# The last norm of a hybrid decoder layer: order of the left half's multiplications, sum of the last squares, and the queue of the last transfers

## The chip, the core and the metric

The kernel runs on one core of a Trainium2 chip. The metric is the device time of one execution in microseconds (us). The core has five engines that take their own instructions in order: TensorE (PE in the profile; its weight loads are PEld), VectorE (DVE), ScalarE (ACT), GpSimd (POOL) and SyncE (SP). SP computes nothing here; it issues the DMA transfers. Engines wait for one another through semaphores.

## What is computed

The reference is one decoder layer over 1024 tokens and 1024 channels. Only its end matters here: the down projection of the MLP is added to the residual, and a norm over the channels of each token follows.

```python
    x = x + (jax.nn.silu(gate) * up) @ w_down
...
    y = xf * lax.rsqrt(jnp.mean(xf * xf, axis=-1, keepdims=True) + EPS)
    return (y * w.astype(jnp.float32)).astype(x.dtype)
```

The kernel keeps the result transposed: channels lie on the 128 partitions, in eight channel tiles `m` = 0 to 7, and tokens lie along the free dimension. So the mean over the channels of a token is a sum over the eight tiles and then over the partitions.

## The kernel before

Most of the kernel is matrix products in three parts (a number is split into a high and a low half, and three products of halves are added). The order of work is written out by hand with the help of a planner, `Weave`, which interleaves streams of work by estimated times; every operation goes through the recorder `Engine`, so that VectorE, ScalarE and GpSimd operations carry line L139 (those of the high-priority recorder L141), and all matrix products carry L189 (function `mm`) or, for transposes through the identity, L193 (function `tp`). On each engine the instructions run in the order in which they are written, as far as this end of the kernel goes.

The MLP's down projection is the function `mlp_down`. It works in four stages with 11 steps each; the tokens are halved (`hh` = 0 is tokens 0 to 511) and the output channels are halved into tiles 0 to 3 and 4 to 7. The last stage makes channel tiles 4 to 7 of token half 0, with four PSUM banks `pa[0]` to `pa[3]` (named `dw` in the trace). By then everything of token half 1 is done, and its last norm is interleaved with the stage. The last five steps of the stage are held back and done bank by bank by `last_product(i, sl)`: 15 matrix products into one bank for 256 tokens `sl`, then `add_to` (VectorE adds the bank to the residual `x1h[4 + i]`), then `complete` (ScalarE squares the sum into `sq`, and VectorE adds the square to `rstdB`, which collects the squares of all eight channel tiles).

The 512 tokens are taken as **left** (0 to 255) and **right** (256 to 511). The order is: the left products of all four banks; the right product of bank 0; then `final_norm(0, left, ...)`, with the right product of bank 1 between its power and its transposes; the right products of banks 2 and 3; and `final_norm(0, right, ...)`.

`final_norm` has these steps: for each 128 tokens a matrix product of `rstdB` with a column of ones (the sum over the partitions); a VectorE multiply and add (`rs`); a power of -1/2 on GpSimd (`rsqrt`); transposes on TensorE that turn the column of 128 factors into a row that stands on all partitions (bank `pb`); and then, for each of the eight channel tiles, one VectorE multiplication (SCALAR_TENSOR_TENSOR) by the norm's weight and by that row, and one transfer of 128 x 256 numbers (128 KB) to the output, `out_xT`, issued by SP. The end of the program waits for the transfers.

So before the change the eight left multiplications stand on VectorE between the add of right bank 1 and the adds of right banks 2 and 3. The right norm's sum over the partitions needs the right squares of all four banks in `rstdB`.

A transfer on the SP queue waits for the multiplication that made its data and for an earlier transfer that used the same one of eight completion semaphores.

Of the kernel before, what the change touches and what calls it, by code (L numbers as in the profile page):

```python
# [7 lines left out]
F32 = mybir.dt.float32  # L8
F32R = mybir.dt.float32r
AF = mybir.ActivationFunctionType  # L10
OP = mybir.AluOpType
# [4 lines left out]
P = 128  # L16
# [8 lines left out]
EPS = 1e-6  # L25
# [119 lines left out]
def hybrid_layer(tc, I, out):  # L145
    nc = tc.nc
    wv = Weave()
    ve = Engine(wv, nc.vector, "vector", 0.07, 0.00105)
    ac = Engine(wv, nc.scalar, "scalar", 0.12, 0.00085)

    uv = Engine(wv, nc.vector, "vector", 0.07, 0.00105, first=tc.high_priority)
    ua = Engine(wv, nc.scalar, "scalar", 0.12, 0.00085, first=tc.high_priority)
    po_ = Engine(wv, nc.gpsimd, "gpsimd", 0.15, 0.0021)
    sy = Engine(wv, nc.sync, "sync", 0.05, 0.00142, 2.2)
    es = ExitStack()
    cp = es.enter_context(tc.tile_pool(name="cp", bufs=1))
    wp = es.enter_context(tc.tile_pool(name="wp", bufs=1))
    lp = es.enter_context(tc.tile_pool(name="lp", bufs=1))
    sp = es.enter_context(tc.tile_pool(name="sp", bufs=1))
# [3 lines left out]
    def tile_(pool, shape, dt, name, tag, bufs):  # L163
        return wv.slot(pool.tile(list(shape), dt, name=name, tag=tag, bufs=bufs), tag, bufs)
# [3 lines left out]
    def A(name, tag, dt=F32, shape=(P, 1024)):  # L168
        if tag in TURNS:
            i = turns[tag] = turns.get(tag, -1) + 1  # L170
            tag = TURNS[tag][i % len(TURNS[tag])]
        return tile_(lp, shape, dt, name, tag, SLOTS[tag])
# [4 lines left out]
    def const(name, shape, src=None):  # L177
        t = cp.tile(list(shape), F32, name=name)
        if src is not None:
            sy.dma_start(t, src)  # L180
        return t
# [3 lines left out]
    def after(inst, anchor, reason="keeps a slot free until it is needed"):  # L185
        tc.add_manual_dep(inst.ins, anchor.ins.name, order, reason=reason)

    def mm(dst, lhs, rhs, us, start=True, stop=True, **kw):
        tc.stamp_issue_order_token(nc.tensor.matmul(dst, lhs, rhs, start=start, stop=stop, **kw).ins, TOKEN)  # L189
        wv.product(us, dst, lhs, rhs)  # L190

    def tp(dst, src, idt=None, us=0.11):
        tc.stamp_issue_order_token(nc.tensor.transpose(dst, src, ident if idt is None else idt).ins, TOKEN)  # L193
        wv.product(us, dst, src)
# [33 lines left out]
    def rsqrt(dst, src, n):  # L228
        po_.tensor_tensor(dst, src, mhalf[:, :n], op=OP.pow)
# [14 lines left out]
    def bank(tag, name="ps"):  # L244
        return tile_(pp_, (P, 512), F32, name, tag, 2)
# [26 lines left out]
    for k in range(KT):  # L272
# [24 lines left out]
        sq = A("sq", "qa")  # L297
# [5 lines left out]
        else:  # L303
            inst = ve.tensor_tensor(acc, acc, sq, op=OP.add)
# [7 lines left out]
    ones = const("ones", [P, 8])  # L312
# [36 lines left out]
    rstdB = const("rstdB", [P, S])  # L349
# [697 lines left out]
    last = {}  # L1047
# [30 lines left out]
    fw = const("fw", [P, KT], I["fw"])  # L1078
# [259 lines left out]
    x1h = {}  # L1338
# [70 lines left out]
    def load_x1(mg, hh):  # L1409
        for m in range(4 * mg, 4 * mg + 4):  # L1410
            if not hh:
                x1h[m] = A("x1h", ("kT", "kT", "dv", "dv", "Xa", "Xa", "Xa", "Xa")[m])
            sy.dma_start(x1h[m][:, half(hh)], xpark[m][:, half(hh)])

    def down(pd, i, op, sl, first, last_):
        (whi, wlo), (hhi, hlo) = op
        c = slice(i * P, (i + 1) * P)
        mm3(pd[:, sl], (whi[:, c], wlo[:, c]), (hhi[:, sl], hlo[:, sl]), first, last_, skip_group_check=True)

    def part(m, hh, sl):  # L1420
        return slice(512 * hh + sl.start, 512 * hh + sl.stop)

    def add_to(pd, m, hh, sl):
        x = x1h[m][:, part(m, hh, sl)]
        ve.tensor_tensor(x, x, pd[:, sl], op=OP.add)

    def complete(m, hh, sl):

        sp_ = part(m, hh, sl)
        x = x1h[m][:, sp_]  # L1430
        sq = tile_(sp, [P, 512], F32, "sq3", "t2", 2)
        ac.activation(sq[:, sl] if m else rstdB[:, sp_], x, AF.Square)
        if m:
            ve.tensor_tensor(rstdB[:, sp_], rstdB[:, sp_], sq[:, sl], op=OP.add)

    def final_norm(hh, sl, tags, between=None):
        n_ = (sl.stop - sl.start) // P
        ss = bank(tags[0])
        for c in range(n_):
            o = 512 * hh + sl.start + c * P  # L1440
            mm(ss[:, c:c + 1], rstdB[:, o:o + P], ones[:, :1], 0.215)
        rs = tile_(sp, [P, 4], F32, "rs3", "rs3", 2)
        ve.tensor_scalar(rs[:, :n_], ss[:, :n_], 1.0 / 1024, EPS, op0=OP.mult, op1=OP.add)
        rsqrt(rs[:, :n_], rs[:, :n_], n_)
        if between is not None:
            between()
        pb = bank(tags[1])
        for c in range(n_):
            tp(pb[:, c * P:(c + 1) * P], rs[:, c:c + 1].to_broadcast([P, P]))
        for m in range(8):  # L1450
            x = x1h[m][:, part(m, hh, sl)]
            ve.scalar_tensor_tensor(x, x, fw[:, m:m + 1], pb[:, :sl.stop - sl.start], op0=OP.mult, op1=OP.mult)
            sy.dma_start(out[m * P:(m + 1) * P, part(m, hh, sl)], x)

    STEPS = [(s_, j) for s_ in range(4) for j in range(HT)]
    XLOADS = {6: (0, 0), 12: (1, 0), 14: (0, 1), 16: (1, 1)}
# [3 lines left out]
    def mlp_down():  # L1460
        yield from wv.until("up")
        whole = slice(0, 512)
        pa = [bank(t, "dw") for t in ("asc", "atr") for _ in range(2)]
        pb = [bank(t, "dw") for t in ("hf", "ch") for _ in range(2)]
        def down_step(stage, j):
            for e, (op, pds) in enumerate(zip(ops[stage, j], (pa, pb))):
                for i in range(4):
                    down(pds[i], i, op, whole, j == 0 and (stage == 0 or (stage, e) == (1, 1)), j == HT - 1)
                if j == HT - 1:
                    mg, hh = ADDS[stage][e]  # L1470
                    for i in range(4):
                        add_to(pds[i], 4 * mg + i, hh, whole)
                        if stage == 0 and e == 1:
                            complete(i, 0, whole)
                        if stage == 2 and e == 1:
                            complete(i, 1, whole)
                    if stage == 2 and e == 1:
                        for i in range(4):
                            complete(4 + i, 1, whole)

        for n, (stage, j) in enumerate(STEPS):
            if n + 1 < len(STEPS):
                prep(*STEPS[n + 1])
            if n in XLOADS:
                load_x1(*XLOADS[n])
            if stage == 3 and j == HT - LAST - 1:
                final_norm(1, whole, ("hf", "ch"), lambda: down_step(stage, j))
            elif stage < 3 or j < HT - LAST:
                down_step(stage, j)

        def last_product(i, sl):
            for j in range(HT - LAST, HT):
                down(pa[i], i, ops[3, j][0], sl, False, j == HT - 1)
            add_to(pa[i], 4 + i, 0, sl)
            complete(4 + i, 0, sl)


        left, right = slice(0, 256), slice(256, 512)
        for i in range(4):
            last_product(i, left)  # L1500
        last_product(0, right)
        final_norm(0, left, ("hf", "ch"), lambda: last_product(1, right))
        for i in (2, 3):
            last_product(i, right)
        final_norm(0, right, ("hf", "ch"))

    wv.add(0, norms())
    wv.add(1, gates())
# [6 lines left out]
    wv.add(0, mixer_splits())  # L1515
    wv.add(8, mlp_up())
    wv.add(8, mlp_down())
    wv.run()
    es.close()
# [58 lines left out]
```

## Time and profile before

| | us |
|---|---|
| median of 3 runs (lowest to highest) | 1223.74 (1222.77 to 1223.82) |
| the profiled execution, its own time | 1223.87 |
| span of that execution, first to last instruction | 1222.1 |
| TensorE busy in the span | 1201.4 |
| VectorE busy | 950.3 |
| ScalarE busy | 574.5 |
| last product of right bank 3 ends | 1210.35 |
| first of the last eight multiplications starts | 1214.85 |
| last of the eight transfers is issued | 1218.74 |

The times of day in the text (1210.35 and so on) are microseconds from the span's start. What the profiled execution takes beside its span, 1223.87 - 1222.1, is outside the first and last instruction. A row of the timeline gives the start, the length from first to last of a merged group, the engine, line and operation, `out<-in`, the count after `x`, and in brackets how long the engine was idle before and what released it. Rows of the same kind are merged when nothing of that engine lies between them, so the length of one is read from the start of the next, or from a narrow window.

### The profile page before, as it was taken

The numbers are of one execution on the slowest core, as the hardware profiler recorded it, in microseconds if no ns is written. First come the engines' busy times: TensorE is split into PE (matmuls) and PEld (weight loads), VectorE is DVE, ScalarE is ACT, GpSimd is POOL, SyncE is SP. The second block draws the span as 40 slices with busy tenths as digits, with TensorE's granted clock in tenths as the row PEclk, the third lists the DMA queues.
The fourth block names the chain that finished last, engine by engine and source line by source line (L and its number), as shares of the span: only waits on it lengthen the run. The fifth ranks groups of instructions, "written<-read, shape, count | busy, mean of one in ns | idle before, by whom it ended". The sixth has DMA issues, their size and how long they took to land.

```text
span 1222.1 us, 18237 instructions
## 1 busy us (share of the span) xinstructions
PE 1201.4 (98%) x7064; PEld 986.3 (81%) x7064; DVE 950.3 (78%) x1458; ACT 574.5 (47%) x1123; POOL 50.1 (4%) x46
## 2 busy tenths in 40 slices
PE   9999999999999999999999999999999999999996
PEld 7878887889777778788888888888888888787886
DVE  7675965566487686668988988989889889899875
ACT  7393344356344453555545544445444444343441
POOL 0211010003100000000000000000000000000000
PEclk9999999999999999999999999999999999999998
DMA  7425252335634213444223123132231496555623
GB/s 228 110 74 168 77 148 88 118 126 163 215 105 121 88 37 101 157 147 155 71 68 104 58 98 99 57 104 65 91 101 55 142 369 238 165 164 181 193 81 138
DMA packets 85799, 154.81 MB, mean 127 GB/s; under 512 B 21168, under 2 KB 36304, under 8 KB 85712
## 3 DMA queue, kind: packets, MB, share of 16 engines
q1 hardware_dynamic: 85712, 153.64, 39.3%
q8 instruction: 55, 0.90, 0.3%
q14 instruction: 32, 0.26, 0.1%
HBM read 117.68 MB, written 35.93 MB: 126 GB/s over the span
## 4 chain that ended last, share of the span: by engine, by line
PE 84%; DVE 8%; DMA 3%; issue 2%; ACT 2%; SPq 0%; POOLq 0%; POOL 0%; DVEq 0%; ACTq 0%
PE ps L189 43%; PE pa L189 20%; PE pc L189 10%; PE dw L189 8%; PE ps L193 3%; DMA wd<-in_wd 3%; DVE pr L139 2%; DVE x1h L139 1%; DVE kT L139 1%; DVE wd L139 1%; ACT dec L139 1%; DMA xt<-in_xT 1%; DVE wlo L139 0%; DVE r L139 0%; ACT sq L141 0%
## 5 line engine op out<-in xcount | busy, mean ns | idle before, releaser
L189 PE MATMUL dw<-pr 128*128 128x512 f32 (+1 forms) x984 | 213.4, 378 | 3.3 <-DVE x1h L139 3.1
L189 PEld LDWEIGHTS dw<-pr 128*128 128x128 f32 x984 | 176.2, 188 | 39.5 <-DVE x1h L139 4.8
L189 PE MATMUL ps<-xhi,whi 128*128 128x512 f32 x384 | 158.7, 413 | 0.0
L189 PE MATMUL ps<-xlo,whi 128*128 128x512 f32 x384 | 150.2, 391 | 0.6 <-DVE xlo L139 0.6
L189 PE MATMUL ps<-xhi,wlo 128*128 128x512 f32 x384 | 150.4, 392 | 0.0
L189 PE MATMUL pa<-T,pair 128*128 128x512 f32 x528 | 127.1, 390 | 0.0
L189 PEld LDWEIGHTS pa<-T,pair 128*128 128x128 f32 x528 | 99.0, 188 | 20.5
L189 PEld LDWEIGHTS ps<-xhi,wlo 128*128 128x128 f32 x384 | 72.1, 188 | 15.7 <-DVE wlo L139 0.2
L189 PEld LDWEIGHTS ps<-xhi,whi 128*128 128x128 f32 x384 | 72.3, 188 | 14.9 <-issue 1.4
L189 PEld LDWEIGHTS ps<-xlo,whi 128*128 128x128 f32 x384 | 72.4, 189 | 12.8 <-DVE xlo L139 1.0
L139 ACT ACTIVATE whi<-wst 128x1024 fp32r<-128x1024 f32 (+2 forms) x42 | 42.9, 1023 | 76.8 <-PE ps L189 53.6
L139 ACT ACTIVATE u<-pa 128x512 f32<-128x512 f32 x44 | 26.4, 599 | 109.5 <-PE pa L189 109.5
L139 DVE SCALAR_TENSOR_TENSOR y<-xu,fcw,y 128x1023 f32<-128x1023 f32 (+1 forms) x44 | 56.4, 1281 | 22.1 <-ACT y L139 22.0
L189 PE MATMUL pa<-B,A 128*128 128x512 f32 x264 | 63.4, 389 | 0.0
L189 PE MATMUL pc<-T,S 128*128 128x512 f32 x264 | 63.4, 389 | 0.0
L189 PE MATMUL pc<-B,pair 128*128 128x512 f32 x264 | 63.4, 389 | 0.0
L189 PE MATMUL pa<-T,S 128*128 128x512 f32 x264 | 63.4, 389 | 0.0
L139 DVE TENSOR_TENSOR wst<-wst 128x512 f32<-128x512 f32 x88 | 60.6, 688 | 0.9
L139 DVE TENSOR_TENSOR wlo<-wst,whi 128x1024 fp32r<-128x1024 f32 (+2 forms) x42 | 49.5, 1177 | 14.5 <-ACT whi L139 14.3
L189 PE MATMUL ps<-B,pair 128*128 128x512 f32 x252 | 60.5, 389 | 0.0
L139 ACT ACTIVATE pr<-wd 128x1024 fp32r<-128x1024 f32 x33 | 34.9, 1059 | 54.5 <-DVE wd L139 32.3
L189 PEld LDWEIGHTS pc<-B,pair 128*128 128x128 f32 x264 | 49.6, 188 | 10.3
(241 smaller groups left out, 2341.8 us busy)
## 6 DMA issues: line engine op xcount, KB each, us to landing
wst<-in_wu SPq DMA_DIRECT2D x44, 512.0 KB, 3.6
wd<-in_wd SPq DMA_DIRECT2D x44, 512.0 KB, 4.1
upark<-y SPq DMA_DIRECT2D x22, 512.0 KB, 3.7
wst<-in_wi SPq DMA_DIRECT2D x21, 512.0 KB, 3.7
r<-upark SPq DMA_DIRECT2D x11, 512.0 KB, 8.1
r<-upark SPq DMA_DIRECT2D x22, 256.0 KB, 7.0
wa<-in_wd SPq DMA_DIRECT2D x22, 256.0 KB, 2.8
wst<-in_wv SPq DMA_DIRECT2D x8, 512.0 KB, 3.7
```

Source lines behind the costliest of these rows:

```text
L139: return getattr(eng, op)(*a, **kw)
L189: tc.stamp_issue_order_token(nc.tensor.matmul(dst, lhs, rhs, start=start, stop=stop, **kw).ins, TOKEN)
L193: tc.stamp_issue_order_token(nc.tensor.transpose(dst, src, ident if idt is None else idt).ins, TOKEN)
```

## The change

`final_norm` is taken apart into `mean_of` (sum over the partitions, multiply and add, power), `turned` (the transposes) and `scale_out` (multiplications and transfers). Token half 1 still goes through `final_norm` as it did. For token half 0:

- The eight left multiplications no longer stand together: channel tiles 0 to 3 follow the add of right bank 1, tiles 4 to 6 follow the add of right bank 2, tile 7 follows the add of right bank 3. An ordering edge (`after`) holds the second and third group behind those adds.
- The right squares of bank 3 are no longer added to `rstdB` on VectorE. `mean_of` gets the tile of squares as `more` and adds a second product with ones per 128 tokens into the same bank.
- The multiply and add of `rs` goes through the high-priority recorder.
- The last eight transfers alternate between SP and ScalarE: even channel tiles on SP, odd ones on a queue of ScalarE (`sa`), which issues no other transfer in the kernel.

In the order in which the changed program stands, VectorE has after the right add of bank 1: four multiplications, the sum of bank 1's squares, the add of bank 2, three multiplications, the sum of bank 2's squares, the add of bank 3, one multiplication, `rs`, and the eight right multiplications. TensorE has two more products with ones; ScalarE has four transfers at its very end, behind the last square. The order before that point is the same on all engines.

```diff
+    sa = Engine(wv, nc.scalar, "actq", 0.05, 0.00142, 2.2)
...
+    def mean_of(hh, sl, tag, more=None):
+        n_ = (sl.stop - sl.start) // P
+        ss = bank(tag)
+        for src, o in ((rstdB, 512 * hh + sl.start), (more, sl.start)):
+            if src is not None:
+                for c in range(n_):
+                    mm(ss[:, c:c + 1], src[:, o + c * P:o + c * P + P], ones[:, :1], 0.215,
+                       src is rstdB and (c == 0 or more is None), src is more or more is None, skip_group_check=True)
+        rs = tile_(sp, [P, 4], F32, "rs3", "rs3", 2)
+        uv.tensor_scalar(rs[:, :n_], ss[:, :n_], 1.0 / 1024, EPS, op0=OP.mult, op1=OP.add)
+        rsqrt(rs[:, :n_], rs[:, :n_], n_)
+        return rs
...
+    def scale_out(hh, sl, pb, ms=range(8), queues=(sy,), anchor=None):
+        for m in ms:
+            x = x1h[m][:, part(m, hh, sl)]
+            inst = ve.scalar_tensor_tensor(x, x, fw[:, m:m + 1], pb[:, :sl.stop - sl.start], op0=OP.mult, op1=OP.mult)
+            if anchor is not None:
+                after(inst, anchor, "the sums of the last banks go first")
+            queues[m % len(queues)].dma_start(out[m * P:(m + 1) * P, part(m, hh, sl)], x)
...
-            complete(4 + i, 0, sl)
-
+            added = add_to(pa[i], 4 + i, 0, sl)
+            return added, complete(4 + i, 0, sl, sl.start > 0 and i == 3)
...
         last_product(0, right)
-        final_norm(0, left, ("hf", "ch"), lambda: last_product(1, right))
-        for i in (2, 3):
-            last_product(i, right)
-        final_norm(0, right, ("hf", "ch"))
+        rs = mean_of(0, left, "hf")
+        last_product(1, right)
+        pl = turned(rs, left, "ch")
+        scale_out(0, left, pl, range(0, 4))
+        third, _ = last_product(2, right)
+        scale_out(0, left, pl, range(4, 7), anchor=third)
+        fourth, more = last_product(3, right)
+        scale_out(0, left, pl, range(7, 8), anchor=fourth)
+        scale_out(0, right, turned(mean_of(0, right, "hf", more), right, "ch"), queues=(sy, sa))
```

More of the change, by code (lines that the diff above doesn't have):

```diff
@@ L1424, in add_to, with complete @@
         x = x1h[m][:, part(m, hh, sl)]
-        ve.tensor_tensor(x, x, pd[:, sl], op=OP.add)
-    def complete(m, hh, sl):
+        return ve.tensor_tensor(x, x, pd[:, sl], op=OP.add)
+    def complete(m, hh, sl, apart=False):
         sp_ = part(m, hh, sl)
@@ L1432, in complete @@
         ac.activation(sq[:, sl] if m else rstdB[:, sp_], x, AF.Square)
+        if apart:
+            return sq
         if m:
             ve.tensor_tensor(rstdB[:, sp_], rstdB[:, sp_], sq[:, sl], op=OP.add)
-    def final_norm(hh, sl, tags, between=None):
[L1437 to L1444, printed above, removed]
+    def mean_of(hh, sl, tag, more=None):
[10 more added lines that the diff above has]
+        return rs
@@ new lines, in turned @@
+    def turned(rs, sl, tag):
+        pb = bank(tag)
+        for c in range((sl.stop - sl.start) // P):
+            tp(pb[:, c * P:(c + 1) * P], rs[:, c:c + 1].to_broadcast([P, P]))
+        return pb
+    def scale_out(hh, sl, pb, ms=range(8), queues=(sy,), anchor=None):
[5 more added lines that the diff above has]
+            queues[m % len(queues)].dma_start(out[m * P:(m + 1) * P, part(m, hh, sl)], x)
@@ L1445, in final_norm @@
+    def final_norm(hh, sl, tags, between=None):
+        rs = mean_of(hh, sl, tags[0])
         if between is not None:
             between()
[L1447 to L1453, printed above, removed]
+        scale_out(hh, sl, turned(rs, sl, tags[1]))
@@ L1493, in last_product @@
                 down(pa[i], i, ops[3, j][0], sl, False, j == HT - 1)
-            add_to(pa[i], 4 + i, 0, sl)
-            complete(4 + i, 0, sl)
+            added = add_to(pa[i], 4 + i, 0, sl)
+            return added, complete(4 + i, 0, sl, sl.start > 0 and i == 3)
         left, right = slice(0, 256), slice(256, 512)
```

## The prediction

> **What bounds the kernel now.** I read the busy shares first, then the chain that ended last, then the timeline of its end.
>
> ```profile
> span 1222.1 us, 18237 instructions
> PE 1201.4 (98%) x7064; PEld 986.3 (81%) x7064; DVE 950.3 (78%) x1458; ACT 574.5 (47%) x1123; POOL 50.1 (4%) x46
> ```
>
> TensorE is busy for 98% of the span, and the change takes no product out of it before the last product of right bank 3. So only the stretch behind that product can become shorter. This is the timeline of that stretch, with its start:
>
> ```profile
> 1206.52 3.83 PE L189 MATMUL dw<-pr 128*128 128x256 f32 x30
> 1206.58 0.42 DVE L139 TENSOR_TENSOR x1h<-x1h,dw 128x256 f32<-128x256 f32 x1 [1.20 <-PE dw L189]
> 1206.92 3.22 DVE L139 SCALAR_TENSOR_TENSOR x1h<-x1h,fw,ps 128x256 f32<-128x256 f32 x8
> 1207.10 0.42 ACT L139 ACTIVATE sq<-x1h 128x256 f32<-128x256 f32 x1 [2.20 <-DVE x1h L139]
> 1210.05 0.42 DVE L139 TENSOR_TENSOR rstdB<-rstdB,sq 128x256 f32<-128x256 f32 x1
> 1210.39 0.75 DVE L139 TENSOR_TENSOR x1h<-x1h,dw 128x256 f32<-128x256 f32 x2
> ...
> 1211.35 0.96 DVE L139 TENSOR_TENSOR rstdB<-rstdB,sq 128x256 f32<-128x256 f32 x2 [0.21 <-ACT sq L139]
> ...
> 1212.45 0.58 PE L189 MATMUL ps<-ones,rstdB 128*128 128x1 f32 x4 [2.10 <-DVE rstdB L139]
> 1213.13 0.16 DVE L139 TENSOR_SCALAR rs<-ps 128x2 f32<-128x2 f32 x1 [0.83 <-PE ps L189]
> 1213.37 0.69 POOL L139 TENSOR_TENSOR rs<-rs,mhalf 128x2 f32<-128x2 f32 x1 [7.76 <-DVE rs L139]
> 1214.12 0.69 PE L193 MATMUL ps<-ident,rs 128*128 128x128 f32 x2 [1.10 <-POOL rs L139]
> 1214.85 3.22 DVE L139 SCALAR_TENSOR_TENSOR x1h<-x1h,fw,ps 128x256 f32<-128x256 f32 x8 [1.56 <-PE ps L193]
> ```
>
> TensorE is done at 1206.52 + 3.83 = 1210.35. From there the path is a string of short steps: the last add, its square, the last sum into `rstdB`, the products with ones, `rs`, the power, the transposes, the eight multiplications. Then SP's transfers end it:
>
> ```profile
> 1215.36 3.77 SPq L139 DMA_DIRECT2D out_xT<-x1h  x8
> 1218.74 0.39 SPq L139 DMA_DIRECT2D out_xT<-x1h  x1
> 1217.60 0.48 DVE L139 SCALAR_TENSOR_TENSOR x1h<-x1h,fw,ps 128x256 f32<-128x256 f32 x1
> SPq L1574 <- DMA out_xT<-x1h: 1.5, 1, 1.5
> DMA to landing us min/median/max: 1.8/1.9/2.0
> ```
>
> The last multiplication starts at 1217.60 and is over at 1218.08, but its transfer is issued at 1218.74: SP is behind VectorE. SP starts one transfer every (1218.74 - 1215.36) / 7 = 0.483 us; VectorE makes one every (1217.60 - 1214.85) / 7 = 0.393 us. After the last issue come the landing (1.9 us from issue; SP's own wait for it, 1.5 us, begins when the issuing is over) and the closing of the program, 1222.1 - 1218.74 = 3.36 us in all.
>
> **Part 1: the order on VectorE.** I replay VectorE's queue with distances from start to start. A multiplication takes (1210.05 - 1206.92) / 8 = 0.391; an add or a sum takes 1210.39 - 1210.05 = 0.34. Beginning at 1206.92: four multiplications to 1208.48, the sum of bank 1 to 1208.82 (its square was done at 1207.52), the add of bank 2 to 1209.16 (its products are the first half of the row of 30, so done near 1206.52 + 1.92 = 1208.44, and the add doesn't wait), three multiplications to 1210.33, the sum of bank 2 to 1210.67, and then the add of bank 3. Its products are done at 1210.35, so VectorE's queue, and not TensorE, sets its start: 1210.67. Before, it was the second of the two adds in one row, 1210.39 + 0.75 - 0.42 = 1210.72. So the new order by itself gives 0.05 us: VectorE stays the last to be ready, with seven multiplications ahead of the add in place of eight, but also one sum more. What the order buys is that the sum of bank 2 is ahead of that add. The eighth multiplication, 1211.01 to 1211.49, runs beside the last square and costs nothing; it would cost something only if it reached to `rs`, near 1212.4. Each left transfer is issued behind its multiplication as before, and the last one now near 1211.5 on SP. With 1.9 us to landing it is gone near 1213.4, ahead of the first right transfer, and SP has nothing else to do. If the cover by VectorE's own queue were gone (products of bank 2 late by more than 1208.82 - 1208.44 = 0.38 us), every tenth would move the last add by a tenth.
>
> **Part 2: the squares of bank 3 go to the ones.**
>
> ```profile
> 1211.23 0.42 ACT L139 ACTIVATE sq<-x1h 128x256 f32<-128x256 f32 x1
> 1211.88 0.43 DVE L139 TENSOR_TENSOR rstdB<-rstdB,sq 128x256 f32<-128x256 f32 x1
> ```
>
> The square starts 1211.23 - 1210.72 = 0.51 us behind its add's start, so now at 1210.67 + 0.51 = 1211.18, and ends at 1211.60. Before, VectorE first finished the sum of bank 2, then began the last sum only at 1211.88 and ended it at 1212.31; the products with ones started 0.14 us later. Now the products over the square start at 1211.60 + 0.14 = 1211.74: they wait on ScalarE and not on VectorE, and I take the same 0.14 for that signal. Behind them on TensorE stand only the transposes. Their sisters over `rstdB` wait for the sum of bank 2 (1210.33 + 0.43 = 1210.76) and take one row of four, 0.58 us, to about 1211.5, so TensorE is free in time. The second row of four costs the same 0.58 as the one it replaces on the path. Everything behind moves with them: 1212.45 - 1211.74 = **0.71 us** earlier. The first right multiplication starts at S = 1214.85 - 0.71 = 1214.14.
>
> One term here has two ends. The transposes may gain speed:
>
> ```profile
> 1206.38 0.38 PE L193 MATMUL ps<-ident,rs 128*128 128x128 f32 x2
> 1212.50:1213.00 0.50, 0.50 (x4) 0.44 (x4) 0.00 (x0) 0.00 (x0) 0.00 (x0) 1.00 0.00 0
> 1213.00:1213.50 0.50, 0.02 (x1) 0.00 (x0) 0.16 (x1) 0.00 (x0) 0.13 (x1) 0.59 0.00 0
> 1213.50:1214.00 0.50, 0.00 (x0) 0.00 (x0) 0.00 (x0) 0.00 (x0) 0.50 (x1) 0.50 0.00 0
> ```
>
> The granted clock (last number but two) fell from 1.00 to 0.50 near 1213.1, and the two transposes took 0.69 us, against 0.38 for the left pair at full clock. In the changed kernel they run near 1213.4, so 0 to 0.31 us is to be had. I take 0, because 1213.4 is behind the fall of the row. The Trainium skill, "TensorE: Matmul & The Clock Gate", section "What's actually happening", says that the gate judges TensorE by a free-running window of about 3.4 us. The fall 2.7 us behind the last dense product agrees with a window that doesn't begin with the idle time; by that rule the window may lie elsewhere in another execution, and the sum would be up to 0.31 us lower.
>
> **Part 3: ScalarE issues half of the last transfers.** The last multiplication ends at S + 3.23 and its transfer could start 1215.36 - 1215.33 = 0.03 us later, at S + 3.26, where SP's eighth started at S + 3.89 (1218.74 - 1214.85). SP and ScalarE each issue one per two multiplications, 0.79 us, and a queue that takes 0.483 keeps up. So **0.63 us**. No row shows a transfer issued by ScalarE. The nearest rows are SP's, this one and the one of all 24 output transfers:
>
> ```profile
> L139 SPq DMA_DIRECT2D out_xT<-x1h x8: 333/394/404, 1215.4 to 1218.7; - x8
> L139 SPq DMA_DIRECT2D out_xT<-x1h x24: 332/396/1517, 1195.7 to 1218.7; - x24
> ```
>
> So the price lies between 0.33 and 1.52 us; I take 0.39, the median of the eight of this very size. A one-time cost on ScalarE's first transfer is hidden up to about 0.9 us: that transfer is due at S + 0.90, and three more at 0.483 are due by S + 2.35 against S + 3.26. Nothing stands behind ScalarE's four transfers on its queue; the squares are ahead of them and long done.
>
> What is late next is the transfer engines:
>
> ```profile
> 1217.50:1218.00 0.50, 0.00 (x0) 0.00 (x0) 0.50 (x2) 0.00 (x0) 0.00 (x0) 0.50 0.81 268
> 1219.00:1219.50 0.50, 0.00 (x0) 0.00 (x0) 0.00 (x0) 0.00 (x0) 0.00 (x0) 0.50 0.81 270
> 1197.50:1198.00 0.50, 0.50 (x6) 0.50 (x5) 0.50 (x2) 0.00 (x0) 0.00 (x0) 1.00 1.04 385
> ```
>
> With an issue every 0.483 us they are 0.81 busy, so one transfer holds them 0.81 x 0.483 = 0.39 us. VectorE's new pace of 0.393 us fills them just to the brim (128 KB in 0.393 us is 334 GB/s; the larger output transfers moved 385). I charge 0.1 us for queueing; from below it is nothing, from above the whole 0.63, if these small rows can't exceed 270 GB/s.
>
> **The sum**, against the profiled execution's own 1223.87: 1223.87 - 0.71 - 0.63 + 0.10 = 1222.63, say 1222.6. The 1.77 us outside the span is left as it is. The profiled execution lies 0.13 over the median of 1223.74, so against the median that is a gain of 1.1 to 1.2 us, about 0.1%. Some 0.2% (2.45 us) is what a measurement of this kernel can tell from no change, so my forecast is "within 0.2%". The forecast's own range is 1222.0 to 1223.2.
>
> **Rivals.**
>
> A. *The second queue gives nothing.* The end is set by what both queues share: one issue per 0.483 us whatever the engine, or engines that carry no more than 270 GB/s in rows of 1 KB. For it: 0.81 is very even in all windows. Against it: 0.81 is not 1.04, and the SP row is 0.39 long and leaves 0.09 of each 0.483 idle. Then the time is 1223.87 - 0.71 = 1223.2. The Trainium skill, "Perfetto Trace Analysis", section "DMA Instruction — HWDGE (DVE, Sync)", says that the block that generates descriptors is shared by two sequencers and locked for exclusive use while it works. By that rule transfers from SP and ScalarE would line up; no run shown has two such queues.
>
> B. *ScalarE's issue is dear, and the kernel gets slower.* Place: the last four instructions of ScalarE. With c us per issue and 0.09 between two, ScalarE's fourth ends at S + 0.90 + 4c + 0.27, where SP's eighth ended at S + 4.28; with 0.71 gained before, the kernel is slower from 4c > 3.82, c > 0.95. At the longest SP row, c = 1.52, it comes to 1223.87 + 2.25 = 1226.1; past 0.2% it goes from c = 1.57. For it: a row of 1.52 exists. Against it: that row stood in a crowd of 256 KB transfers, and the median of 24 is 0.396.
>
> C. *The clock stays up*: another 0.31 off, 1222.3.
>
> D. *The change doesn't do what it says*: VectorE's steps that wait leave gaps, the last add comes half a microsecond later than I replay, and ScalarE's signal is slow; parts 1 and 2 then give about 0.1 in place of 0.71, and the time is 1222.63 + 0.61 = 1223.2.
>
> **Chances.** Forecast 0.60, A 0.15, C 0.10, B 0.08, D 0.07. The range for 8 in 10: downwards 1221.5, which is the lowest run shown (1222.77) with the sum of 1.24 taken off; upwards 1224.3, which covers A and D, and B up to c = 1.05. Faster by over 0.2% (under 1221.3) gets 0.08, from the low end of C and the forecast; slower by over 0.2% (above 1226.2) gets 0.07, most of B; within 0.2% the rest, 0.85.
>
> **What the changed profile would show.** Part 1: the add of bank 3 within 0.1 us of 1210.7, preceded by the sum of bank 2. Part 2: the products with ones over `sq` at 0.14 us behind the square, `rs` near 1212.4, the first right multiplication near 1214.1. Part 3: four SP and four ScalarE rows alternating, the last one within 0.05 us behind the last multiplication, an engine share near 1 in the last windows. A shows as longer rows on both queues or a share that stays at 0.81; B as long ScalarE rows, the last one behind the last multiplication by more than 1.6 us; C as a transpose row near 0.38. I'd be wrong altogether if something ahead of 1206 moves, where the order is unchanged, or if the closing of the program, 3.36 us from the last issue, takes longer with a second queue to close.

## The result

| | before | changed |
|---|---|---|
| median of 20 runs each, us (lowest to highest) | 1223.43 (1221.93 to 1224.93) | 1221.25 (1219.49 to 1222.90) |
| ratio changed to before, 95% interval | | 0.9987 (0.9981 to 0.9993) |
| span of the profiled execution | 1222.1 | 1219.5 |

The changed kernel is faster by 0.13% (0.07 to 0.19%): 0.9 to 2.3 us, where 1.1 to 1.2 was forecast. The difference lies under the 0.2% that was called visible, and clear of no change. The median itself, 1221.25, is a little below 1221.5, the low end of the range for 8 in 10. But the kernel before also lies lower over its 20 runs (1223.43) than over the first three of them (1223.74), and the ratio put on 1223.74 gives 1222.2.

Single runs of one kernel spread over 3 us, so where the time went is read inside the profiles, as distances from one event that no variant touches: the start of the add of right bank 1 (1206.58 before, 1206.09 changed). This is the timeline of the changed kernel from there, without the rows of weight loads, of the first two squares and of SP:

```profile
1206.02 3.83 PE L190 MATMUL dw<-pr 128*128 128x256 f32 x30
1206.09 0.42 DVE L139 TENSOR_TENSOR x1h<-x1h,dw 128x256 f32<-128x256 f32 x1 [1.19 <-PE dw L190]
1206.43 1.65 DVE L139 SCALAR_TENSOR_TENSOR x1h<-x1h,fw,ps 128x256 f32<-128x256 f32 x4
1207.99 0.42 DVE L139 TENSOR_TENSOR rstdB<-rstdB,sq 128x256 f32<-128x256 f32 x1
1208.33 0.41 DVE L139 TENSOR_TENSOR x1h<-x1h,dw 128x256 f32<-128x256 f32 x1
1208.66 1.26 DVE L139 SCALAR_TENSOR_TENSOR x1h<-x1h,fw,ps 128x256 f32<-128x256 f32 x3
1209.84 0.41 DVE L139 TENSOR_TENSOR rstdB<-rstdB,sq 128x256 f32<-128x256 f32 x1
1210.17 0.41 DVE L139 TENSOR_TENSOR x1h<-x1h,dw 128x256 f32<-128x256 f32 x1
1210.40 0.58 PE L190 MATMUL ps<-ones,rstdB 128*128 128x1 f32 x4 [0.55 <-DVE rstdB L139]
1210.51 0.47 DVE L139 SCALAR_TENSOR_TENSOR x1h<-x1h,fw,ps 128x256 f32<-128x256 f32 x1
1210.68 0.42 ACT L139 ACTIVATE sq<-x1h 128x256 f32<-128x256 f32 x1 [1.43 <-DVE x1h L139]
1211.15 0.61 PE L190 MATMUL ps<-ones,sq 128*128 128x1 f32 x4 [0.17 <-ACT sq L139]
1211.86 0.16 DVE L141 TENSOR_SCALAR rs<-ps 128x2 f32<-128x2 f32 x1 [0.89 <-PE ps L190]
1212.10 0.70 POOL L139 TENSOR_TENSOR rs<-rs,mhalf 128x2 f32<-128x2 f32 x1 [6.98 <-DVE rs L141]
1212.85 0.43 PE L194 MATMUL ps<-ident,rs 128*128 128x128 f32 x2 [1.10 <-POOL rs L139]
1213.32 3.22 DVE L139 SCALAR_TENSOR_TENSOR x1h<-x1h,fw,ps 128x256 f32<-128x256 f32 x8 [1.30 <-PE ps L194]
1214.23 2.69 ACTq L139 DMA_DIRECT2D out_xT<-x1h  x4
1216.58 0.34 ACTq L139 DMA_DIRECT2D out_xT<-x1h  x1
```

The reader is to see three things. The last products with ones no longer stand behind a sum on VectorE. The first group of four still waits for the sum of bank 2, but is done by 1210.98; the second waits for ScalarE's square and starts 0.05 us after it (1211.15 - 1210.68 - 0.42). The transposes took 0.43 us, not 0.69. And the last transfer is issued 3.26 us behind the first multiplication (1216.58 - 1213.32), where before it was 3.89. The granted clock and the transfer engines, in windows of the changed kernel (the last three numbers are granted clock, engine share and GB/s):

```profile
1212.50:1213.00 0.50, 0.15 (x1) 0.15 (x2) 0.00 (x0) 0.00 (x0) 0.30 (x1) 1.00 0.00 0
1213.00:1213.50 0.50, 0.29 (x2) 0.04 (x1) 0.18 (x1) 0.00 (x0) 0.00 (x0) 1.00 0.00 0
1215.50:1216.00 0.50, 0.00 (x0) 0.00 (x0) 0.50 (x2) 0.00 (x0) 0.00 (x0) 0.50 1.02 334
1217.00:1217.50 0.50, 0.00 (x0) 0.00 (x0) 0.00 (x0) 0.00 (x0) 0.00 (x0) 0.50 1.04 344
```

The clock was still 1.00 at the transposes. The transfer engines now run at a share of 1.0 and 334 to 344 GB/s, where they stood at 0.81 and 270.

All profiles of this study, as distances in us. "Sums" is the start of the last products with ones, S the first right multiplication, both counted from the add of right bank 1:

| kernel | add of bank 3 | sums | rs | transposes | S | S to last issue | last issue to end |
|---|---|---|---|---|---|---|---|
| before | 4.14 | 5.87 | 6.55 | 0.69 | 8.27 | 3.89 | 3.36 |
| before, once more | 4.13 | 5.87 | 6.56 | 0.69 | 8.27 | 3.89 | 3.36 |
| changed | 4.08 | 5.06 | 5.77 | 0.43 | 7.23 | 3.26 | 2.93 |
| changed, once more | 4.08 | 5.05 | 5.77 | 0.69 | 7.49 | 3.25 | 2.93 |
| parts 1 and 2 alone | 4.08 | 5.06 | 5.77 | 0.43 | 7.23 | 3.89 | 3.29 |
| part 3 alone | 4.13 | 5.87 | 6.55 | 0.43 | 8.01 | 3.25 | 3.18 |
| part 1 alone | 4.08 | 5.61 | 6.39 | 0.69 | 8.11 | 3.88 | 3.38 |
| part 2 alone | 4.13 | 5.77 | 6.46 | 0.43 | 7.92 | 3.90 | 3.29 |
| before, more products | 4.13 | 5.77 | 6.49 | 0.43 | 7.95 | 3.87 | 3.37 |
| before, more SP code | 4.13 | 5.87 | 6.55 | 0.69 | 8.27 | 3.88 | 3.06 |
| changed, all on ScalarE | 4.09 | 5.06 | 5.78 | 0.43 | 7.24 | 3.97 | 2.98 |
| two behind | 3.80 | 4.78 | 5.50 | 0.64 | 7.16 | 3.26 | 2.93 |
| two behind, more products | 3.80 | 4.78 | 5.50 | 0.43 | 6.96 | 3.26 | 2.93 |

The add of bank 3 is the second of a merged row in the old order, taken as that row's start, plus its length, less the 0.42 of one add. The last issue is read from a narrow window of each trace. The end of the span is taken to the nanosecond from the trace files, since the views round it to 0.1 us.

### The profile page after: what moved, and what is told of

Its sections match the earlier page's. It is cut to its first block, busy times and chain, and to the rows that moved or that the text cites. A ratio compares the mean times of both kernels' runs of the same rounds, so it can differ in the third digit from the quotient of the medians.

```text
span 1219.5 us, 18242 instructions
## 1 busy us (share of the span) xinstructions
PE 1202.0 (99%) x7068; PEld 987.1 (81%) x7068; DVE 949.8 (78%) x1457; ACT 574.5 (47%) x1123; POOL 50.1 (4%) x46
## 4 chain that ended last, share of the span: by engine, by line
PE 84%; DVE 7%; DMA 4%; issue 2%; ACT 2%; SPq 0%; POOLq 0%; POOL 0%; DVEq 0%; ACTq 0%
PE ps L190 44%; PE pa L190 19%; PE pc L190 10%; PE dw L190 8%; DMA wd<-in_wd 3%; PE ps L194 3%; DVE pr L139 2%; DMA r<-upark 1%; DVE x1h L139 1%; DVE kT L139 1%; DVE wd L139 1%; ACT dec L139 1%; PE warm L190 1%; DVE wlo L139 0%; DVE r L139 0%
## 5 line engine op out<-in xcount | busy, mean ns | idle before, releaser
L190 PEld LDWEIGHTS pa<-T,S 128*128 128x128 f32 x264 | 49.5, 188 | 10.3
```

## The experiments

The theory after the result: parts 1 and 2 gain 0.78 us and need each other; part 3 gains 0.63 us by issuing and some 0.4 us more in the closing of the program; the length of the transposes is set by the granted clock, which falls at a time that differs between executions and belongs to neither kernel. The rivals stand with each run.

### Parts 1 and 2 alone

```diff
-        scale_out(0, right, turned(mean_of(0, right, "hf", more), right, "ch"), queues=(sy, sa))
+        scale_out(0, right, turned(mean_of(0, right, "hf", more), right, "ch"))
```

> The changed kernel with all transfers on SP, so parts 1 and 2 alone. From the add of right bank 1 to the first right multiplication the kernel before takes 8.27 us and the changed one 7.23. Both theories expect 7.2 to 7.3 here. From that multiplication to the end before takes 7.25 us and the changed kernel 6.18. Theory Q (the second queue shortens the end, by the issuing and by the closing of the program): 7.25 again, about 1.0 us off in all. Rival E (the closing is 0.4 us shorter by chance or because of parts 1 and 2): near 6.8, about 1.5 us off. From the issue of the last transfer to the end: Q 3.36 as before, E 2.9 as in the changed kernel.

Measured: S at 7.23, and 7.18 us from there to the end; 3.29 from the last issue to the end. Ratio to before 0.9991 (0.9982 to 1.0000). The closing is that of before: theory Q, not E.

### Part 3 alone

The edit is against the changed kernel. Only the lines that come in are shown; `complete(4 + i, 0, sl)` is as before too.

```diff
+        final_norm(0, left, ("hf", "ch"), lambda: last_product(1, right))
+        for i in (2, 3):
+            last_product(i, right)
+        scale_out(0, right, turned(mean_of(0, right, "hf"), right, "ch"), queues=(sy, sa))
```

> The kernel before with the last eight transfers alternating between SP and ScalarE, so part 3 alone. Both theories expect 8.27 us from the add of right bank 1 to the first right multiplication. Theory Q: 6.2 from there to the end, with 2.9 from the last issue to the end, so about 1.1 us off in all. Rival E: 6.6 with 3.36 from the last issue, 0.6 off.

Measured: 6.43 us from S to the end, 3.18 from the last issue, ratio 0.9987 (0.9978 to 0.9996). That lies between the two numbers expected: the second queue does shorten the closing (by 0.2 us), but less than in the changed kernel. S came at 8.01 and not 8.27, which both theories missed: the transposes took 0.43 us here, in the same order of work as before. It was the first sign that the clock, and not the change, sets their length.

```profile
1213.12 0.43 PE L194 MATMUL ps<-ident,rs 128*128 128x128 f32 x2 [1.10 <-POOL rs L139]
```

### Part 1 alone, and part 2 alone

Part 1 alone is the changed kernel with `complete(4 + i, 0, sl)` as before, `mean_of(0, right, "hf")` and all transfers on SP. Part 2 alone, again with only the lines that come in:

```diff
+        final_norm(0, left, ("hf", "ch"), lambda: last_product(1, right))
+        last_product(2, right)
+        _, more = last_product(3, right)
+        scale_out(0, right, turned(mean_of(0, right, "hf", more), right, "ch"))
```

> Part 1 alone: the left multiplications apart as in the changed kernel, the last squares summed on VectorE, all transfers on SP. By the prediction's replay: add of bank 3 4.09 us behind the add of bank 1 (before 4.14), its square, then the last sum at once, products with ones at 1212.27 - 1206.58 = 5.69 (before 5.87), first right multiplication 0.18 us earlier at 8.09 if the clock falls as before, 7.8 if it stays up. Rival (the order gives all of the gain and the ones nothing): 7.3.

> Part 2 alone: the old order of VectorE, the last squares summed by ones, all transfers on SP. The sum of bank 2 then ends at 1211.78 and its four rows of products with ones take 0.58 us to 1212.5, the four over the last squares follow: nothing to 0.35 us gained if the order is needed as well, so 7.9 to 8.3 us from the add of bank 1 to the first right multiplication. Rival (the ones give the gain alone): 7.2 to 7.5.

Measured: `rs` at 6.39 and at 6.46, against 6.55 before and 5.77 with both. S was 8.11 with the clock down and 7.92 with it up. So one part alone gains 0.16 and 0.09 us, and the two together 0.78. Neither rival holds. The traces show why. Part 1 alone:

```profile
1209.25 0.42 DVE L139 TENSOR_TENSOR rstdB<-rstdB,sq 128x256 f32<-128x256 f32 x1
1209.59 0.41 DVE L139 TENSOR_TENSOR x1h<-x1h,dw 128x256 f32<-128x256 f32 x1
...
1210.10 0.42 ACT L139 ACTIVATE sq<-x1h 128x256 f32<-128x256 f32 x1 [1.43 <-DVE x1h L139]
1210.55 0.42 DVE L139 TENSOR_TENSOR rstdB<-rstdB,sq 128x256 f32<-128x256 f32 x1 [0.15 <-ACT sq L139]
1211.12 0.68 PE L190 MATMUL ps<-ones,rstdB 128*128 128x1 f32 x4 [1.84 <-DVE rstdB L139]
```

The sum of bank 2 is early, at 1209.25, but the last square still goes through VectorE (1210.55) before the ones may start. Part 2 alone:

```profile
1208.21 0.75 ACT L139 ACTIVATE sq<-x1h 128x256 f32<-128x256 f32 x2 [3.38 <-DVE x1h L139]
1208.66 0.42 DVE L139 TENSOR_TENSOR rstdB<-rstdB,sq 128x256 f32<-128x256 f32 x1 [0.21 <-ACT sq L139]
1209.23 0.58 PE L190 MATMUL ps<-ones,rstdB 128*128 128x1 f32 x4 [1.57 <-DVE rstdB L139]
1209.67 0.59 PE L190 MATMUL ps<-ones,sq 128*128 128x1 f32 x4
```

Here the last square is done at 1208.96, but the sum of bank 2 ends only at 1209.08, and its own four products stand ahead of the ones over the square. Each part takes away one of two waits that end nearly together.

### Before, with more products to hold the clock

```diff
         for i in (2, 3):
             last_product(i, right)
+        spare = bank("asc", "dw")
+        wide = ops[3, HT - 1][0]
+        for k in range(12):
+            mm(spare[:, :256], wide[0][0][:, :P], wide[1][0][:, :256], 0.13, k == 0, k == 11, skip_group_check=True)
```

> The kernel before with 12 more products of 256 columns on TensorE behind the last product of right bank 3, into a spare bank that nobody reads, so that TensorE is busy until about 1.6 us later. Theory K (the transposes' length is the granted clock and nothing that the change does): the sums over the ones start 5.87 us behind the add of bank 1 as before, the transposes take 0.43 us in place of 0.69, the first right multiplication comes at 8.0 in place of 8.27. Rival (the transposes are slow for another reason, for example because the row is first read there): 0.69 and 8.27.

Measured: transposes 0.43, S at 7.95, as theory K has it. One profile can't show this by itself, since the transposes took 0.43 also in five of the eleven profiles without products added. What shows it are the times at which the granted clock fell, which the trace files hold: the transposes took 0.69 us in the five profiles in which it fell before they started, 0.64 in the one in which it fell 0.08 us behind their start, and 0.43 in the seven in which it fell 0.38 us or more behind it. Here it fell 5.9 us behind the last product of right bank 3, and without products added never later than 5.0. The last 0.06 us are not the transposes': the sums began 0.06 us behind VectorE's last sum, where it took 0.14 before, and the step to `rs` took 0.04 more.

### Before, with more code on SP

```diff
+        spare = cp.tile([P, 128], F32, name="spare")
+        for k in range(16):
+            after(sy.dma_start(spare[:, 8 * k:8 * k + 8], I["sel"]), ops["load"], "late")
         left, right = slice(0, 256), slice(256, 512)
```

`ops["load"]` is the last load of weights, so the 16 stand between it and the output.

> The kernel before with 16 small loads more on SP (4 KB each, into a tile that nobody reads) between the last weights and the first output transfer, where SP waits anyway. They shift the place of SP's last instructions in its code. Theory F (the closing of the program is longer with all transfers on SP because SP's code has a load of instructions to fetch near the end, the one row of queue q14 about 0.5 us before the end): the fetch goes from the end to an earlier time, and from the last issue to the end it takes 2.9 to 3.2 us in place of 3.36. Rival W (it is longer because one queue's last transfers take longer to be waited for): 3.3 to 3.4 as before, with or without a fetch.

Measured: 3.06 us from the last issue to the end in place of 3.36 (in both profiles of before), with S and the issues where they were. The queue q14 loads instructions. Before, one of its loads is the only transfer in the last 0.6 us of the span. The first row is that window of the kernel before (engine share and GB/s last), the second the like window of the kernel with more SP code, which has none:

```profile
1221.50:1222.10 0.60, 0.00 (x0) 0.00 (x0) 0.00 (x0) 0.00 (x0) 0.00 (x0) 0.50 0.05 14
```

```profile
1220.10:1220.60 0.50, 0.00 (x0) 0.00 (x0) 0.00 (x0) 0.00 (x0) 0.00 (x0) 0.50 0.00 0
```

In the trace with more SP code the last q14 load in the span starts 10.54 us before the end, where SP waits for data anyway. In the six traces with a load in the last half microsecond the closing takes 3.29 to 3.38 us, in the seven without, 2.93 to 3.18. So theory F is right that the place in SP's code costs the 0.3 us here; theory W's 3.3 to 3.4 didn't come.

But SP isn't waiting for that load. The trace files also hold SP's short waiting instructions, which the timeline leaves out. Before, the wait for the last transfer is over at 1220.65, and SP's next instruction starts at 1221.00: a pause of 0.35 us, where the same step takes 0.04 in the kernel with more SP code. The load starts at 1221.63, when the pause has been over for 0.62 us. All six traces with a load have the pause at this place, 0.34 to 0.35 us. So pause and load both go with the place in the code; what SP does in the pause, no trace shows.

The changed kernel has four transfers less on SP, and the page counts one load less (first row before, second changed):

```profile
q14 instruction: 32, 0.26, 0.1%
```

```profile
q14 instruction: 31, 0.25, 0.1%
```

The page counts the span alone. The load isn't saved: it starts 0.57 us behind the end of the span, and SP's steps up to the end have no gap longer than in the kernel with more SP code. A pause may be hidden in SP's last wait for GpSimd, 0.38 us in both. In the trace of part 3 alone SP does pause, a few instructions later than before (1219.32 to 1219.68), and the load starts 0.32 us behind the end; the closing of 3.18 us there, against 2.93, goes with that pause.

### All eight last transfers on ScalarE

```diff
-        scale_out(0, right, turned(mean_of(0, right, "hf", more), right, "ch"), queues=(sy, sa))
+        scale_out(0, right, turned(mean_of(0, right, "hf", more), right, "ch"), queues=(sa,))
```

> The changed kernel with all eight last transfers on ScalarE. If ScalarE's queue is like SP's (the prediction's value): an issue every 0.48 us, the last at 3.9 us behind the first right multiplication, engine share 0.81. If it is dearer (rival B of the prediction): a longer distance. From the last issue to the end: 2.9 to 3.2 us by theory F, since SP's code is shorter still; 3.3 to 3.4 by theory W.

```profile
L139 ACTq DMA_DIRECT2D out_xT<-x1h x8: 374/406/412, 1212.5 to 1216.0; - x8
```

ScalarE's issue takes 0.406 us where SP's took 0.394, one every 0.49 us, the last at S + 3.97. Rival B's dear issue isn't there. The closing took 2.98 us, without the pause: against theory W again, since here one queue carries all eight, as in the kernel before.

### Two multiplications behind the last add

```diff
-        scale_out(0, left, pl, range(4, 7), anchor=third)
+        scale_out(0, left, pl, range(4, 6), anchor=third)
...
-        scale_out(0, left, pl, range(7, 8), anchor=fourth)
+        scale_out(0, left, pl, range(6, 8), anchor=fourth)
```

> The changed kernel with two left multiplications behind the add of right bank 3 in place of one (four, two and two). In the changed kernel the add of bank 3 starts 0.32 us behind the end of its products, because VectorE is still at the third multiplication and the sum of bank 2. With one multiplication less ahead of it the add comes 0.28 us earlier, and so does the first right multiplication: 6.95 us behind the add of bank 1 in place of 7.23; the end 0.28 us earlier, which is inside the interval. Rival (something else holds the chain, for example the sum of bank 2 and its products): 7.23 or later.

```profile
1208.71 0.42 DVE L139 TENSOR_TENSOR rstdB<-rstdB,sq 128x256 f32<-128x256 f32 x1
1209.16 0.42 DVE L139 TENSOR_TENSOR x1h<-x1h,dw 128x256 f32<-128x256 f32 x1
...
1210.14 0.61 PE L190 MATMUL ps<-ones,sq 128*128 128x1 f32 x4 [0.28 <-ACT sq L139]
1210.86 0.16 DVE L141 TENSOR_SCALAR rs<-ps 128x2 f32<-128x2 f32 x1 [0.49 <-PE ps L190]
1211.10 0.69 POOL L139 TENSOR_TENSOR rs<-rs,mhalf 128x2 f32<-128x2 f32 x1 [6.70 <-DVE rs L141]
1211.85 0.64 PE L194 MATMUL ps<-ident,rs 128*128 128x128 f32 x2 [1.10 <-POOL rs L139]
1212.52 3.22 DVE L139 SCALAR_TENSOR_TENSOR x1h<-x1h,fw,ps 128x256 f32<-128x256 f32 x8 [1.51 <-PE ps L194]
```

The add of bank 3 moved from 4.08 to 3.80 and `rs` from 5.77 to 5.50, as expected. S came at 7.16 and not 6.95: in this execution the clock fell 0.08 us behind the start of the transposes (0.64 us). Ratio to before 0.9985 (0.9976 to 0.9994).

### The changed kernel again, and two behind with more products

Before and the changed kernel ran once more without an edit. The third kernel is the one above, with six products like those of the clock experiment between the last sums and the transposes.

> The kernel before once more, for what its own end varies by. Theory F and K together: 6.55 us from the add of bank 1 to rs whatever the clock; transposes 0.69 or 0.43 by where the clock falls, so the first right multiplication at 8.27 or 8.01; one fetch 0.5 us before the end, and 3.3 to 3.4 us from the last issue to the end.

> The changed kernel once more, beside the next one on the same chip. 5.77 us from the add of bank 1 to rs; the first right multiplication at 7.23 with the clock up or 7.46 to 7.49 with the clock down; from there to the end 6.2. Against the kernel before 0.998 to 0.9995.

> The version with two left multiplications behind the add of bank 3, and six more products of 256 columns on TensorE between the sums over the ones and the transposes, into a spare bank that nobody reads, to hold the granted clock up. By theory K the transposes take 0.43 us and the first right multiplication comes at 6.95 us behind the add of bank 1, 0.28 ahead of the changed kernel, 1.3 ahead of the kernel before. If six products are too few for the clock: 7.16 as without them. The rival for the time: the six products end late and hold up the transposes, 7.1 or more with the transposes at 0.43.

```profile
1210.60 0.16 DVE L141 TENSOR_SCALAR rs<-ps 128x2 f32<-128x2 f32 x1 [0.89 <-PE ps L190]
1210.84 0.70 POOL L139 TENSOR_TENSOR rs<-rs,mhalf 128x2 f32<-128x2 f32 x1 [6.97 <-DVE rs L141]
1211.59 0.69 PE L194 MATMUL ps<-ident,rs 128*128 128x128 f32 x2 [1.10 <-POOL rs L139]
1212.32 3.22 DVE L139 SCALAR_TENSOR_TENSOR x1h<-x1h,fw,ps 128x256 f32<-128x256 f32 x8 [1.56 <-PE ps L194]
```

These rows are of the changed kernel's second profile. With the same code as in the first, the transposes took 0.69 us and S came at 7.49. So at equal clock the changed kernel's S is 0.78 us earlier (8.27 to 7.49 with the clock down; with it up, from the 8.01 of part 3 alone, which has the old order, to 7.23). The ratio was 0.9982 (0.9973 to 0.9991). The kernel with six more products reached S at 6.96 with transposes of 0.43, and a ratio of 0.9984 (0.9975 to 0.9993) in runs on the same chip as 0.9982 for the changed kernel. Inside the profile it is 0.27 to 0.53 us ahead of the changed kernel up to S; in whole runs the two can't be told apart. That the six products held the clock isn't shown: it fell 4.2 us behind the last product of right bank 3, and without products added it fell 2.2 to 5.0 us behind it.

## Why the prediction was right, and where its sizes were off

The forecast, faster by about 0.1% and so "within 0.2%", was right, and so was its mechanism in parts 1, 2 and 3; the size of the closing was off.

**Part 1.** The add of bank 3 was replayed at 4.09 us behind the add of bank 1 (1210.67 - 1206.58) and came at 4.08. VectorE's queue, not TensorE, set it; the version with two multiplications behind shows it: with one less ahead of it the add came 0.28 us earlier, 0.04 us behind the end of its products.

**Part 2.** 0.71 was forecast up to S and 0.78 measured at equal clock. The products with ones started 0.05 us behind ScalarE's square, where 0.14 was read behind VectorE's sum; whether the engine makes the difference stays open, since the clock experiment saw 0.06 behind VectorE. From there on the chain was 0.02 to 0.03 us longer. That the two parts only work together was in the replay, which needed both, and in the remark that the order brings the sum of bank 2 ahead of the add. But the prediction gave the order 0.05 us "by itself" and booked all the rest under part 2. Alone, part 2 is worth 0.09.

**The clock term** was taken as 0 with up to 0.31 open: the measured difference of the transposes is 0.26 us. As a difference between the two kernels 0 is right. But in the changed kernel's first profile the clock did stay up, so rival C came about there, by luck. The reason given for 0 was weak: that 1213.4 "is behind the fall of the row" supposed that the fall comes at one place in every execution. It doesn't: the transposes took 0.43 us in the kernel with part 3 alone, which has the order of before, and 0.43 and 0.69 in two executions of the changed kernel. The Trainium skill's rule ("TensorE: Matmul & The Clock Gate", section "What's actually happening"), a window that runs on its own, fits these profiles. They also bear out its length of about 3.4 us: by the trace files the clock stood at 1.00 for 1208.32 us in eight of the thirteen profiles and for 1204.91 in the other five, with nothing between, and the two differ by 3.41.

**Part 3.** The issuing gave 0.63 us, as forecast to the hundredth. The 0.10 charged for queueing wasn't needed: the last packet was through 1.41 us behind the last issue in both kernels. Rival A held that a share of 0.81 might be the transfer engines' limit for such rows; they went to 1.0.

Rival A's other form, the shared generator of the Trainium skill ("Perfetto Trace Analysis", section "DMA Instruction — HWDGE (DVE, Sync)"), changed nothing here. But the runs don't test it: with rows of 0.33 and 0.34 us begun 0.39 us apart on the two queues, no two issues ever overlapped.

**The step that was mis-sized** is the tail: "the closing of the program, 1222.1 - 1218.74 = 3.36 us in all" was carried over whole. It fell to 2.93. Of the 0.43 us, 0.31 are SP's pause behind the last landing (0.35 us in place of 0.04), shown by moving it away in the kernel before, where the closing then took 3.06. The other 0.12 go with two short steps of 0.05 and 0.06 us that SP in the kernel before takes behind the landing, where in the changed kernel it already stands at the second of them when the data land; that is read from the traces and not tested. The shorter last issue (0.34 us in place of 0.39) gives nothing: the data land 1.88 and 1.87 us behind its start.

The sum with the measured sizes is 0.78 + 0.63 + 0.43 = 1.84 us, against 1.24. In the profiles with the clock down, the add of right bank 1 is 15.51 us from the end before and 13.67 changed, which is the same 1.84. The intervals of the two comparisons, 0.9 to 2.3 and 1.1 to 3.3 us, hold both numbers, so it is the profiles and not the runs that say 1.84.

## What to carry to other kernels

Replay the queue of the engine that is last, with start-to-start distances from the trace, before pricing an order: here it gave the moved instruction's place to 0.01 us. Where two waits end nearly together, price the edits together; alone they gave 0.16 and 0.09 us, together 0.78. When one engine issues transfers slower than another makes their data, a second issuing queue is worth the lag of the last issue, and the end of the program deserves a look of its own: its length isn't a constant of the chip but may hold a pause of the issuing engine that moves with the number of instructions ahead of it.

## What the runs showed that was not expected

- The closing of the program, from the last issue to the end, takes 3.29 to 3.38 us where SP pauses for 0.34 to 0.35 us behind the last landing, 2.93 to 3.06 where no pause shows, and 3.18 in the one trace where it comes a few instructions later. A load on the instruction queue follows 0.6 to 0.7 us behind the pause.
- SP's issue of a 128 KB transfer takes 0.33 us when it is let alone and 0.39 to 0.41 when one follows on another; ScalarE's takes 0.34 and 0.41.
- Behind the last dense products the granted clock fell before the transposes or at their start in six of the eleven profiles without products added to hold it, of both orders of work; where it was down, two transposes took 0.64 to 0.69 us in place of 0.43. The stretch of full clock had one of two lengths, 3.41 us apart.
